# Where sequence 1's attention operands and squares are made: at the end of layer 0's second MLP product, or during the first blocks of q, k and v

## The chip, the cores and the metric

One Trainium2 chip, one core. The metric is the device time of one execution in microseconds (us), lower is better. The kernel before takes 1733.64 us, the median of three executions (1732.1 to 1736.89).

## The reference, cut to what matters

Two sequences, `x_prompt` and `x_sample` (each 512 tokens of 1024 features, fp32), go through the same trunk of two layers: a Fourier mixer and an MLP, then attention and an MLP. The place of interest is where layer 0 ends and layer 1's attention begins:

```python
def trunk(x, ...):
    x = x + fourier_mix(rms_norm(x, fourier_norm[0]), fourier_w_out[0])
    x = x + sq_relu_mlp(rms_norm(x, mlp_norm[0]), mlp_w_up[0], mlp_w_down[0])
    x = x + gqa_attention(rms_norm(x, attn_norm[0]), attn_w_qkv[0], ...)   # qkv = h @ w_qkv
    ...

def rms_norm(x, g):
    return x * rsqrt(mean(x * x, axis=-1) + EPS) * g
```

So each sequence needs the sum of its squares per token, and its activations times the gain `attn_norm`, before q, k and v are complete.

## The kernel before, in words

Activations are held transposed: features on the 128 partitions, 512 tokens along the row. `xt(q, fo)` is block `fo` (of 8) of sequence `q`, and the tile `xs[q, m]` holds the two blocks `2m` and `2m+1`. Every fp32 operand of a product is split into a high half and a low remainder, and each product is three matmuls (high by high, high by low, low by high). ScalarE (ACT) makes the high half and VectorE (DVE) the remainder: L82 and L83 for plain operands, L86 and L87 for operands that are scaled on the way.

The second MLP product of layer 0 (`second_product`) multiplies blocks of the hidden activations of both sequences by sums of weight blocks, in the manner of Strassen. Its last group runs over the output blocks `m` = 0 to 3. Each `m` is five products of 12 matmuls, in the order t1, t3, t2, b22, t4 (L818); DVE adds each one to the residual (L1065), then adds the shared part `e[m]` (L1229 for sequence 0, L1230 for sequence 1), and calls `ready(m)`. Meanwhile DVE also forms and splits the next block's weights (L1132 to L1140, L83). `late()` starts the loads and splits of the first four weight tiles of q, k and v.

`ready(m)` works for both sequences. For each of the two feature blocks, `make_h` writes the attention operand (the activation times the gain, as two halves: L86 on ACT, L87 on DVE), and `square` squares the block on ACT (L157) and adds it to a running sum on GpSimd (POOL, L159). `put_away` writes `xs[q, m]` to memory (`park`, L186, queue of SP).

The projection has three column groups: `cg` = 2 is k and v, 0 and 1 are q. A block `(cg, q, t)` is the product of 128 tokens `t` of sequence `q` by 512 columns, 8 feature blocks by 3 matmuls (L77 to L79). The four blocks `(2, 0, t)` are first done for feature blocks 0 to 5 (`begun`, 72 matmuls). Then `token_scale(0)` sums the squares over features with tiny matmuls (`sums`, L165) and takes the reciprocal root in small steps on DVE and ACT (L131 to L137). The loop then finishes the four blocks with feature blocks 6 and 7 (24 matmuls), and `token_scale(1)` is called after the first of them. Then come the blocks `(2, 1, t)`.

Each k/v block is finished on the other engines by one chain: ACT scales it out of PSUM (L1492), v is split (L86, L87), k is squared per head (L1380), its root is taken (L131 to L137), ACT applies it (L1397), DVE rotates it (L1403, L1406) and POOL adds the two parts (L1408). After the change these lines stand one lower or higher (L1493, L1379, L1396, L1402, L1405, L1407). The first transposes of k (L1418) stand before block `(2, 1, 2)`.

The order on each engine is not written out here. A scheduler places the instructions from the order in which the code issues them, and at run time each engine takes its own in that fixed order. Within the last group only the order of the matmuls is pinned by hand (`manual_schedule` with PE).

Of the kernel before, what the change touches and what calls it, by code (L numbers as in the profile page):

```python
# [21 lines left out]
NSEQ = 2  # L22
NT = S // P
KC = D // P
# [16 lines left out]
def trunk_kernel(ctx, tc, x_in, xt_in, y_out, dcos, dsin, feat, rope, gfour, gcol, grow, gfin,  # L41
# [19 lines left out]
    def slot(shape, dt):  # L61
        return act.tile(shape, dt, tag="u4", name=nm("u"))

    def tm(shape=(P, 512), dt=F32):
        return tmp.tile(list(shape), dt, tag="t2", name=nm("t"))
# [19 lines left out]
    def split_scaled(dst_hi, dst_lo, src, scale):  # L85
        nc.scalar.activation(dst_hi, src, AF.Copy, scale=scale)  # L86
        nc.vector.scalar_tensor_tensor(dst_lo, src, scale, f32(dst_hi), ALU.mult, ALU.subtract)  # L87
# [22 lines left out]
    def load_w(src, eng=nc.vector, parts=1, home=own):  # L110
        raw = load_raw(src)
        w = home()
        for i in range(parts):
            sl = slice(i * 1024 // parts, (i + 1) * 1024 // parts)
            split(w[0][:, sl], w[1][:, sl], raw[:, sl], eng)
        return w
# [32 lines left out]
    def xt(q, fo):  # L149
        return xs[q, fo // 2][:, fo % 2]  # L150

    def square(q, fo, n=512):

        if fo == 0:
            acc[q] = tm()
        s = tm() if fo else acc[q]
        nc.scalar.activation(s[:, :n], xt(q, fo)[:, :n], AF.Square)  # L157
        if fo:
            nc.gpsimd.tensor_add(acc[q][:, :n], acc[q][:, :n], s[:, :n])  # L159
# [17 lines left out]
    def make_h(q, fo, g0):  # L177

        h = slot([P, 2, 512], F32R)
        split_scaled(h[:, 0], h[:, 1], xt(q, fo), gc[:, g0 + fo : g0 + fo + 1])  # L180
        return h
# [3 lines left out]
    def put_away(q, i):  # L185
        nc.sync.dma_start(park[q, i], xs[q, i])  # L186
# [859 lines left out]
    def second_product(l, blocks, rows, late=lambda: None, ready=lambda m: None):  # L1046
# [179 lines left out]
        def finish(m):  # L1226
            left[m] -= 1
            if left[m] == 0:
                nc.vector.tensor_add(xs[0, m][:, 1], xs[0, m][:, 1], e[m])  # L1229
                nc.vector.tensor_add(xs[1, m], xs[1, m], e[m].unsqueeze(1).broadcast_to([P, 2, 512]))  # L1230
                ready(m)
# [100 lines left out]
    hT, rs, wkv = [[], []], [], []  # L1332

    def token_scale(q):
        r = sm.tile([P, NT], F32, tag="rs", name=nm("rs"), bufs=2)
        ss, room = sums(q)
        rsqrt(r, ss, NT, 1.0 / D, room)
        rs.append(r)
# [2 lines left out]
        for _ in range(2):  # L1341
            wkv.append(load_w(w_qkv[2, len(wkv)], home=lent))

    def ready(m):
        for q in range(NSEQ):
            for fo in range(2 * m, 2 * m + 2):
                hT[q].append(make_h(q, fo, KC))
                square(q, fo)
            put_away(q, m)

    second_product(0, blocks, rows, late, ready)

    gb = tm((P, 4, HD))
# [13 lines left out]
    def qkv(cg, q, t, ws, k0=0, k1=KC, o=None):  # L1367
        o = ps() if o is None else o
        cols = slice(t * P, (t + 1) * P)
        for k in range(k0, k1):  # L1370
            w = ws[k // 2]
            c = (k % 2) * 512
            mm3(o, hT[q][k][:, 0, cols], hT[q][k][:, 1, cols],
                w[0][:, c : c + 512], w[1][:, c : c + 512], k == 0, k == KC - 1)
        return o
# [7 lines left out]
    def norm_rope(raw, nh, table, ts, outs, ss=None, step=None, eng=nc.vector):  # L1383

        n = nh * len(ts)
        step = nh if step is None else step
        if ss is None:
            ss = small(n)
            head_squares(raw, 0, n, ss)
        r = small(n)  # L1390
        rsqrt(r[:, :n], ss[:, :n], n, 1.0 / HD)
        yield
        for h0 in range(0, n, step):
            t = ts[h0 // nh]
            x, t1, t2 = [tm((P, step, HD)) for _ in range(3)]
            for i in range(step):  # L1396
                nc.scalar.activation(x[:, i], raw[:, (h0 + i) * HD : (h0 + i + 1) * HD],  # L1397
                                     AF.Copy, scale=r[:, h0 + i : h0 + i + 1])

            def every(ap):  # L1400
                return ap.unsqueeze(1).broadcast_to([P, step, ap.shape[-1]])

            eng.tensor_mul(t1, x, every(table[:, 0, t]))  # L1403
            for b in range(2):
                sl, other = slice(b * 64, b * 64 + 64), slice(64 - b * 64, 128 - b * 64)  # L1405
                nc.vector.tensor_mul(t2[:, :, sl], x[:, :, other], every(table[:, 1, t, sl]))  # L1406
            for i in range(0, step, 2):  # L1407
                nc.gpsimd.tensor_add(outs[(h0 + i) // 2].rearrange("p (h d) -> p h d", h=2),  # L1408
                                     t1[:, i : i + 2], t2[:, i : i + 2])
            yield  # L1410
# [3 lines left out]
    def transpose_k(q):  # L1414
        for h in range(NKV):
            pt = ps()
            for t in range(NT):
                nc.tensor.transpose(pt[:, t * P : (t + 1) * P],  # L1418
                                    kr[q][:, t, h * HD : (h + 1) * HD], ident)
            kk = slot([P, 2, 512], F32R)  # L1420
            split(kk[:, 0], kk[:, 1], pt)
            kT[q, h] = kk

    def transpose_q(q, h):
        pt = ps()
        c = (h % 2) * HD
        for t in range(NT):
            nc.tensor.transpose(pt[:, t * P : (t + 1) * P], qr[q, h // 2][:, t, c : c + HD], ident)
        qT = slot([P, 2, 512], F32R)
        split(qT[:, 0], qT[:, 1], pt)  # L1430
        return qT
# [37 lines left out]
    for cg in (2, 0, 1):  # L1469
        ws = wkv if cg == 2 else [load_w(w_qkv[cg, u], home=own if u < 2 else lent) for u in range(4)]  # L1470
        for q in range(NSEQ):
            if cg == 2:
                vt[q] = (slot([P, NT, 256], F32R), slot([P, NT, 256], F32R))
                kr[q] = slot([P, NT, 256], F32)
            else:
                for i in range(2):
                    qr[q, 2 * cg + i] = slot([P, NT, 256], F32)
            for t in range(NT if (cg, q) != (1, 1) else 2):
                if (cg, q, t) in transposes:
                    transpose_k(transposes[cg, q, t])  # L1480
                if (cg, q, t) == (1, 1, 1):
                    first = transpose_q(0, 0)
                if (cg, q) == (2, 0):
                    o = qkv(cg, q, t, ws, KC - 2, KC, begun[t])
                else:
                    o = qkv(cg, q, t, ws)
                if (cg, q, t) == (2, 0, 0):
                    token_scale(1)
                r = rs[q][:, t : t + 1]
                if cg == 2:  # L1490
                    raw = tm((P, 256))
                    nc.scalar.activation(raw, o[:, :256], AF.Copy, scale=r)  # L1492
                    split_scaled(vt[q][0][:, t], vt[q][1][:, t], o[:, 256:], r)  # L1493
                    todo = norm_rope(raw, NKV, rt["k"], [t], [kr[q][:, t]])
                else:
                    raw = tm()
                    nc.scalar.activation(raw, o, AF.Copy, scale=r)
                    todo = norm_rope(raw, 4, rt["q"], [t], [qr[q, 2 * cg + i][:, t] for i in range(2)])
                for _ in todo:
                    pass  # L1500
# [324 lines left out]
```

## Time and profile before

| what | value |
|---|---|
| median of three executions | 1733.64 us |
| the profiled execution's own time | 1733.91 us |
| its span, first instruction to last | 1732.1 us |
| PE (TensorE matmuls) busy | 1696.8 us, 98% of the span |
| DVE, ACT, POOL busy | 1246.8, 858.1, 332.8 us |
| granted TensorE clock, mean | 0.996 of full speed |

In the rows of the profile a line begins with the start in us and the duration, then engine, line of the code, operation and tiles; `x12` is the number of instructions that were merged into the row, and the bracket at its end is the idle time of that engine before it and what ended it. PE is busy nearly all the time, so the time of the kernel is the work of PE plus the moments when PE waits.

### The profile page before, as it was taken

The numbers are of one execution on the slowest core, as the hardware profiler recorded it, in microseconds if no ns is written. First come the engines' busy times: TensorE is split into PE (matmuls) and PEld (weight loads), VectorE is DVE, ScalarE is ACT, GpSimd is POOL, SyncE is SP. The second block draws the span as 40 slices with busy tenths as digits, with TensorE's granted clock in tenths as the row PEclk, the third lists the DMA queues.
The fourth block names the chain that finished last, engine by engine and source line by source line (L and its number), as shares of the span: only waits on it lengthen the run. The fifth ranks groups of instructions, "written<-read, shape, count | busy, mean of one in ns | idle before, by whom it ended". The sixth has DMA issues, their size and how long they took to land. (4 is left out here: it accounts for less than half of the span.)

```text
span 1732.1 us, 21931 instructions
## 1 busy us (share of the span) xinstructions
PE 1696.8 (98%) x7855; PEld 1400.0 (81%) x7855; DVE 1246.8 (72%) x1840; ACT 858.1 (50%) x1516; POOL 332.8 (19%) x302
## 2 busy tenths in 40 slices
PE   8999999999999999999999999999999999999997
PEld 6887777888788888788877888788788888888886
DVE  7779777546877879975588834687755579787965
ACT  5666444445432435446687714654544554344234
POOL 1320443232000001322234303114332200000004
PEclk9999999999999999999999999999999999999999
DMA  9732555449653635421100213235543587465322
GB/s 316 197 120 100 182 183 177 147 173 346 238 206 122 213 131 203 162 88 38 36 25 1 98 49 122 103 108 182 185 158 140 198 311 257 145 213 193 119 74 97
DMA packets 103751, 266.59 MB, mean 154 GB/s; under 512 B 10185, under 2 KB 10185, under 8 KB 103642
## 3 DMA queue, kind: packets, MB, share of 16 engines
q1 hardware_dynamic: 87482, 233.21, 38.3%
q10 hardware_dynamic: 14112, 25.70, 3.9%
q0 software_dynamic: 2048, 6.29, 1.8%
q8 instruction: 61, 1.00, 0.2%
q14 instruction: 48, 0.39, 0.1%
HBM read 190.18 MB, written 73.92 MB: 152 GB/s over the span
## 5 line engine op out<-in xcount | busy, mean ns | idle before, releaser
L818 PE MATMUL ps<-u,w 128*128 128x512 f32 x4704 | 1079.3, 390 | 7.0 <-DVE w L83 5.0
L818 PEld LDWEIGHTS ps<-u,w 128*128 128x128 f32 x4704 | 883.3, 188 | 195.1 <-DVE w L83 7.4
L82 ACT CAST w<-raw 128x1024 fp32r<-128x1024 f32 (+1 forms) x226 | 220.8, 981 | 447.7 <-PE ps L818 272.4
L83 DVE TENSOR_TENSOR w<-raw,w 128x1024 fp32r<-128x1024 f32 (+1 forms) x226 | 263.7, 1169 | 72.2 <-ACT w L82 71.8
L159 POOL TENSOR_TENSOR t<-t,t 128x512 f32<-128x512 f32 (+1 forms) x56 | 80.2, 1435 | 732.8 <-ACT t L157 677.0
L83 DVE TENSOR_TENSOR u<-u,u 128x1024 fp32r<-128x1024 f32 x132 | 157.8, 1223 | 26.7 <-ACT u L82 26.1
L82 ACT CAST u<-u 128x1024 fp32r<-128x1024 f32 x132 | 132.3, 1044 | 70.0 <-PE ps L818 47.5
L77 PE MATMUL ps<-u,u 128*128 128x512 f32 (+2 forms) x388 | 150.2, 388 | 0.8 <-DVE u L83 0.4
L1065 DVE TENSOR_TENSOR u<-ps,u 128x512 f32<-128x512 f32 x160 | 109.9, 688 | 54.4 <-PE ps L818 53.8
L78 PE MATMUL ps<-u,u 128*128 128x512 f32 (+2 forms) x388 | 144.9, 373 | 1.1 <-DVE u L83 1.1
L79 PE MATMUL ps<-u,u 128*128 128x512 f32 (+2 forms) x388 | 144.4, 372 | 0.0
L818 PE MATMUL ps<-u,u 128*128 128x512 f32 x528 | 129.4, 396 | 8.3 <-DVE t L902 8.2
L818 PEld LDWEIGHTS ps<-u,u 128*128 128x128 f32 x528 | 98.8, 190 | 34.4 <-issue 7.8
L926 POOL TENSOR_TENSOR u<-u 128x512 f32<-128x512 f32 x28 | 36.5, 1304 | 421.9 <-ACT u L834 421.9
L83 DVE TENSOR_TENSOR u<-ps,u 128x512 fp32r<-128x512 f32 (+4 forms) x122 | 75.3, 635 | 19.5 <-ACT u L82 18.0
L78 PEld LDWEIGHTS ps<-u,u 128*128 128x128 f32 x388 | 73.4, 189 | 13.2 <-DVE u L83 3.1
L77 PEld LDWEIGHTS ps<-u,u 128*128 128x128 f32 x388 | 73.5, 190 | 12.2 <-ACT u L82 1.0
L79 PEld LDWEIGHTS ps<-u,u 128*128 128x128 f32 x388 | 73.1, 189 | 12.5
L82 ACT CAST u<-ps 128x512 fp32r<-128x512 f32 (+4 forms) x122 | 64.9, 548 | 25.4 <-PE ps L79 10.9
L801 DVE TENSOR_TENSOR u<-ps,u 128x512 f32<-128x512 f32 (+1 forms) x48 | 30.9, 645 | 64.7 <-PE ps L79 64.7
L891 DVE TENSOR_TENSOR t<-ps,u 128x512 f32<-128x512 f32 x30 | 20.7, 690 | 69.3 <-PE ps L818 64.0
L79 PE MATMUL ps<-u,w 128*128 128x512 f32 (+2 forms) x192 | 65.5, 341 | 2.5 <-DVE w L545 2.5
(233 smaller groups left out, 2006.6 us busy)
## 6 DMA issues: line engine op xcount, KB each, us to landing
raw<-w_up SPq DMA_DIRECT2D x82, 512.0 KB, 4.3
u<-spill_t SPq DMA_DIRECT2D x60, 512.0 KB, 6.1
raw<-w_sum SPq DMA_DIRECT2D x56, 512.0 KB, 3.8
u<-spill_b SPq DMA_DIRECT2D x45, 512.0 KB, 5.5
spill_t<-u SPq DMA_DIRECT2D x87, 256.0 KB, 2.0
spill_b<-t ACTq DMA_DIRECT2D x60, 256.0 KB, 2.9
raw<-w_row SPq DMA_DIRECT2D x28, 512.0 KB, 4.6
park<-u SPq DMA_DIRECT2D x24, 512.0 KB, 2.7
```

The source lines that it names most:

```text
L77: nc.tensor.matmul(out, lh, rh, start=first, stop=False)
L78: nc.tensor.matmul(out, lh, rl, start=False, stop=False)
L79: nc.tensor.matmul(out, ll, rh, start=False, stop=last)
L82: nc.scalar.copy(dst_hi, src)
L83: eng.tensor_sub(dst_lo, src, f32(dst_hi))
L159: nc.gpsimd.tensor_add(acc[q][:, :n], acc[q][:, :n], s[:, :n])
L801: nc.vector.tensor_add(x[:, :n], o[:, :n], x[:, :n])
L818: nc.tensor.matmul(o, w[x][:, sl], h[k][y], start=first and k + i == 0, stop=k == n - 1 and i == 2, skip_group_check=not first)
L891: nc.vector.tensor_add(u2, ob, t[:, 0])
L926: eng.tensor_sub(t[:, 0], b12, b11)
L1065: nc.vector.tensor_add(x, o, x)
```

## The change

`ready` takes the sequence as an argument and does sequence 0 alone at the end of the second product. For sequence 1 it is called from the projection's loop: after block `(2, 0, t)` it makes the operands, squares and write-out of tile `xs[1, t]`. `token_scale(1)`, which reads the sum of all squares of sequence 1, moves from after block `(2, 0, 0)` to after block `(2, 0, 3)`. No instruction of the computation is added or taken away.

```diff
-    def ready(m):
-        for q in range(NSEQ):
-            for fo in range(2 * m, 2 * m + 2):
-                hT[q].append(make_h(q, fo, KC))
-                square(q, fo)
-            put_away(q, m)
+    def ready(m, q=0):
+        for fo in range(2 * m, 2 * m + 2):
+            hT[q].append(make_h(q, fo, KC))
+            square(q, fo)
+        put_away(q, m)
...
                     o = qkv(cg, q, t, ws)
-                if (cg, q, t) == (2, 0, 0):
+                if (cg, q) == (2, 0):
+                    ready(t, 1)
+                if (cg, q, t) == (2, 0, 3):
                     token_scale(1)
```

DVE, at block m = 2 and the start of m = 3 of the last group. `u_5778` and `u_5784` are operands of sequence 1 (its tile is `u_3902`), `u_5771` is one of sequence 0. `w_5858` is the split weight that the first product of m = 3 waits for, `w_5934` that of its second product. Before:

```order
L87 SCALAR_TENSOR_TENSOR u_5771<-u_3679,gc,u_5771 128x512
L1134 TENSOR_TENSOR raw_5824<-raw_5824,raw_5822 128x512
L87 SCALAR_TENSOR_TENSOR u_5778<-u_3902,gc,u_5778 128x512
L87 SCALAR_TENSOR_TENSOR u_5784<-u_3902,gc,u_5784 128x512
L1065 TENSOR_TENSOR u_4019<-ps_5826,u_4019 128x512
L1140 TENSOR_TENSOR raw_5822<-raw_5822,raw_5854 128x512
L83 TENSOR_TENSOR u_5794<-raw_5791,u_5793 128x1024
L1065 TENSOR_TENSOR t_3745<-ps_5840,t_3745 128x512
L83 TENSOR_TENSOR u_5800<-raw_5797,u_5799 128x1024
L83 TENSOR_TENSOR w_5858<-raw_5854,w_5858 128x1024
```

After (the names are numbered anew: `u_5759` is sequence 0's operand, `w_5833` and `w_5896` are the two weights, `t_3745` and `u_4019` are sums of block m = 2):

```order
L87 SCALAR_TENSOR_TENSOR u_5759<-u_3679,gc,u_5759 128x512
L1134 TENSOR_TENSOR raw_5799<-raw_5799,raw_5797 128x512
L83 TENSOR_TENSOR u_5769<-raw_5766,u_5768 128x1024
L1065 TENSOR_TENSOR u_4019<-ps_5801,u_4019 128x512
L83 TENSOR_TENSOR u_5775<-raw_5772,u_5774 128x1024
L83 TENSOR_TENSOR w_5833<-raw_5829,w_5833 128x1024
L1065 TENSOR_TENSOR t_3745<-ps_5815,t_3745 128x512
L1140 TENSOR_TENSOR raw_5797<-raw_5797,raw_5829 128x512
L87 SCALAR_TENSOR_TENSOR u_5869<-u_3683,gc,u_5869 128x512
L83 TENSOR_TENSOR w_5850<-raw_5797,w_5850 128x512
L1065 TENSOR_TENSOR u_4019<-ps_5783,u_4019 128x512
L83 TENSOR_TENSOR w_5896<-raw_5799,w_5896 128x1024
```

The two operands of sequence 1 are gone from here, and the weight of m = 3 now stands ahead of the addition that reads the product t2 of m = 2 (`t_3745`) instead of behind it.

POOL, where layer 1 begins. `t_5626` is the running sum of squares of sequence 0, `t_5638` that of sequence 1 before and `t_6108` after; L1408 (after: L1407) is the last step of k for one block of tokens. Before:

```order
L159 TENSOR_TENSOR t_5626<-t_5626,t_6017 128x512
L159 TENSOR_TENSOR t_5638<-t_5638,t_6024 128x512
L159 TENSOR_TENSOR t_5638<-t_5638,t_6030 128x512
L1408 TENSOR_TENSOR u_6149<-t_6192,t_6193 128x256
L1408 TENSOR_TENSOR u_6149<-t_6227,t_6228 128x256
```

After:

```order
L159 TENSOR_TENSOR t_6108<-t_6108,t_6113 128x512
L1407 TENSOR_TENSOR u_6098<-t_6138,t_6139 128x256
L159 TENSOR_TENSOR t_6108<-t_6108,t_6155 128x512
L159 TENSOR_TENSOR t_6108<-t_6108,t_6161 128x512
L1407 TENSOR_TENSOR u_6098<-t_6186,t_6187 128x256
L159 TENSOR_TENSOR t_6108<-t_6108,t_6203 128x512
L159 TENSOR_TENSOR t_6108<-t_6108,t_6209 128x512
L1407 TENSOR_TENSOR u_6098<-t_6234,t_6235 128x256
L159 TENSOR_TENSOR t_6108<-t_6108,t_6251 128x512
L159 TENSOR_TENSOR t_6108<-t_6108,t_6257 128x512
L1407 TENSOR_TENSOR u_6098<-t_6297,t_6298 128x256
```

Six of the seven additions for sequence 1 now stand between the last steps of the four k blocks, the last two behind that of the third block.

PE, at the end of the k/v blocks of sequence 0. `ps_6157` (after: `ps_6262`) is the sum over features of sequence 1's squares, `ps_6308` is block `(2, 1, 0)`, the first of sequence 1. Before, with matmuls of the same kind left out:

```order
L165 MATMUL ps_6133<-ones,t_5626 128x2 x4
L77 MATMUL ps_6056<-u_5928,u_6008 128x512
...
L79 MATMUL ps_6056<-u_5928,u_6014 128x512
L165 MATMUL ps_6157<-ones,t_5638 128x2 x4
L77 MATMUL ps_6075<-u_5928,u_6008 128x512
...
L79 MATMUL ps_6113<-u_5928,u_6014 128x512
L77 MATMUL ps_6308<-u_5793,u_5635 128x512
```

After:

```order
L165 MATMUL ps_6082<-ones,t_5626 128x2 x4
L77 MATMUL ps_6005<-u_5890,u_5970 128x512
...
L79 MATMUL ps_6062<-u_5890,u_5976 128x512
L165 MATMUL ps_6262<-ones,t_6108 128x2 x4
L77 MATMUL ps_6308<-u_5768,u_6105 128x512
```

The tiny matmuls that read sequence 1's sum of squares move from behind the first finished block to the last place before block `(2, 1, 0)`, and they read the sum that POOL now completes behind the third k block.

## The prediction

> **What bounds the kernel now.** The page gives the busy time of the engines, and the waits of PE say what it waited for.
>
> ```profile
> PE 1696.8 (98%) x7855; PEld 1400.0 (81%) x7855; DVE 1246.8 (72%) x1840; ACT 858.1 (50%) x1516; POOL 332.8 (19%) x302
> ```
>
> ```profile
> PE ps L818 <- DVE w L83: 5.0, 4, 2.3
> PE ps L1418 <- POOL u L1408: 0.7, 1, 0.7
> ```
>
> PE is the bound everywhere, so any edit counts by what it adds to or takes from PE's waits. The timeline of PE shows the waits near the change.
>
> ```profile
> 671.62 44.81 PE L818 MATMUL ps<-u,w 128*128 128x512 f32 x197
> 717.95 3.01 PE L818 MATMUL ps<-u,w 128*128 128x512 f32 x12 [1.51 <-DVE w L83]
> 723.28 12.33 PE L818 MATMUL ps<-u,w 128*128 128x512 f32 x46 [2.32 <-DVE w L83]
> 735.45 0.39 PE L77 MATMUL ps<-u,u 128*128 128x512 f32 x1
> ...
> 751.77 0.95 PE L165 MATMUL ps<-ones,t 128*128 128x2 f32 x8
> 752.58 0.49 PE L77 MATMUL ps<-u,u 128*128 128x512 f32 x1
> ...
> 754.06 0.95 PE L165 MATMUL ps<-ones,t 128*128 128x2 f32 x8
> 754.87 0.48 PE L77 MATMUL ps<-u,u 128*128 128x512 f32 x1
> ...
> 758.82 0.39 PE L79 MATMUL ps<-u,u 128*128 128x512 f32 x1
> 759.04 0.39 PE L77 MATMUL ps<-u,u 128*128 128x512 f32 x1
> ```
>
> PE runs without a pause to 716.4, then waits twice, both times for a split weight of the last block, m = 3. `begun` starts at 735.45; its 72 matmuls end at 751.77, so a warm matmul takes 16.32 / 72 = 0.227. The sums stand at 751.77 and 754.06, and the 24 matmuls that finish the four blocks end at 759.04, where block (2, 1, 0) starts. The table by stage (length, PE busy, PEld, DVE, ACT, POOL, then granted clock) says what the waits did to the clock.
>
> ```profile
> 716.40:718.00 1.60, 0.09 (x2) 0.05 (x1) 1.60 (x2) 0.00 (x0) 0.42 (x1) 1.00 0.75 161
> 720.90:723.20 2.30, 0.07 (x1) 0.00 (x0) 2.30 (x4) 1.02 (x2) 0.00 (x0) 1.00 0.95 376
> 723.20:726.70 3.50, 3.42 (x9) 2.64 (x10) 3.50 (x5) 3.50 (x7) 3.14 (x2) 0.55 1.02 368
> 759.00:800.00 41.00, 40.31 (x186) 33.32 (x186) 26.06 (x95) 25.74 (x97) 7.32 (x10) 1.00 0.08 26
> ```
>
> DVE is busy through both waits, so its queue is the cause; behind the second one PE had 0.55 of its clock for 3.5 us. From 759 to 800 PE idles 0.69 in all: what is lost earlier cannot be won back there.
>
> **Term 1, the two waits go.** DVE's rows (701 to 724) show what stood ahead of the weights.
>
> ```profile
> 708.12 3.48 DVE L87 SCALAR_TENSOR_TENSOR u<-u,gc,u 128x512 fp32r<-128x512 f32 x2
> ...
> 715.60 2.30 DVE L83 TENSOR_TENSOR w<-raw,w 128x1024 fp32r<-128x1024 f32 x1
> ...
> 720.16 0.68 DVE L1065 TENSOR_TENSOR u<-ps,u 128x512 f32<-128x512 f32 x1
> 720.76 0.73 DVE L87 SCALAR_TENSOR_TENSOR u<-u,gc,u 128x512 fp32r<-128x512 f32 x1
> 721.42 0.68 DVE L1229 TENSOR_TENSOR u<-u,t 128x512 f32<-128x512 f32 x1
> 722.02 1.21 DVE L83 TENSOR_TENSOR w<-raw,w 128x1024 fp32r<-128x1024 f32 x1
> ```
>
> The L87 pair at 708.12 is sequence 1's and leaves. The split that ended the first wait (715.60) then stands ahead of the addition of t2 of m = 2, two products or more before PE needs it; the one that ended the second (722.02) moves ahead of L1065, L87 and L1229. Each then has over 3 us to spare, and what is late next is PE's own work. Without waits the 60 matmuls of m = 3 run from 716.28 (the last start of the first row plus 0.227) for 60 x 0.227 = 13.61, and `begun` starts at 729.89, not 735.45: **-5.56**. This is 1.51 + 2.32 of waiting and some 1.7 of slow clock. The loads of w_qkv follow their buffers' release, which comes earlier; SP writes sequence 1's tiles as before, by the same four transfers; one load of w_qkv now stands ahead of sequence 0's last write and of the load of the gains (L1354), which the rotation of the first k block needs, long after. If a weight is late after all, this term falls towards 0.
>
> The Trainium skill ("TensorE: Matmul & The Clock Gate", Part 1: The HAM clock gate) lets PE fall to half clock after an idle window of about 3.4 us; here it fell after 2.32, so the trace disagrees on the length, though a wait of 2.31 earlier in it left the clock at 1.00:
>
> ```profile
> 267.11 3.01 PE L818 MATMUL ps<-u,u 128*128 128x512 f32 x12 [2.31 <-DVE t L902]
> ```
>
> ```profile
> 267.20:271.00 3.80, 3.80 (x17) 1.00 0.84 299
> ```
>
> By the Trainium skill's window this term would be an estimated -3.83, the waits alone, and the sum 1.7 higher.
>
> **Term 2, PE now waits for sequence 1's squares.** PE takes its queue in order, and L165 for sequence 1 is the last item before block (2, 1, 0): every matmul of that block and all later ones are queued behind it. It waits for POOL's last L159, which stands behind the last step (L1407) of the third k block. That step ends a chain that begins when the first block leaves PSUM. Rows of before (ACT, then POOL):
>
> ```profile
> 754.31 0.47 ACT L1492 ACTIVATE t<-ps,rs 128x256 f32<-128x256 f32 x1 [0.75 <-PE ps L79]
> ...
> 758.61 0.46 ACT L1492 ACTIVATE t<-ps,rs 128x256 f32<-128x256 f32 x1
> ...
> 762.46 0.46 ACT L1492 ACTIVATE t<-ps,rs 128x256 f32<-128x256 f32 x1
> ```
>
> ```profile
> 767.15 0.74 POOL L1408 TENSOR_TENSOR u<-t,t 128x256 f32<-128x256 f32 x1 [2.93 <-DVE t L1406]
> ```
>
> The three blocks leave PSUM one after another, though PE has all of them by 759.04: the chain is serial on ACT, some 3.85 a block, and takes 767.89 - 754.31 = 13.58 to the end of the third L1408. Before, only the transposes at 771 waited for it. Its start moves with PE, to 754.31 - 5.56 = 748.75, so with nothing added it ends at 762.33. But sequence 1's work is now threaded into it:
>
> ```profile
> 704.63 0.72 ACT L86 ACTIVATE u<-u,gc 128x512 fp32r<-128x512 f32 x1 [3.83 <-DVE u L1229]
> 705.26 0.62 ACT L157 ACTIVATE t<-u 128x512 f32<-128x512 f32 x1
> 705.78 0.71 ACT L86 ACTIVATE u<-u,gc 128x512 fp32r<-128x512 f32 x1
> ```
>
> Start to start, L86 costs ACT 0.63 and L157 0.52. Between the first and the second block ACT has two of each: +2.30. Inside the second block's root DVE has four L87 (0.74 each, by the row at 720.76): +2.96. Between the second and the third block ACT has two L157: +1.04. Third step done: 762.33 + 6.30 = 768.63. Then POOL makes its last two L159, by the page's group
>
> ```profile
> L159 POOL TENSOR_TENSOR t<-t,t 128x512 f32<-128x512 f32 (+1 forms) x56 | 80.2, 1435 | 732.8 <-ACT t L157 677.0
> ```
>
> 2 x 1.435 = 2.87, to 771.50, and L165 takes 754.87 - 754.06 = 0.81. Block (2, 1, 0) starts at 772.31 instead of 759.04: **+13.27**, term 1 already in it. PE itself would have been there by 753.5, so it idles some 18 us.
>
> **Term 3, the clock.** After such an idle stretch PE restarts slow. By the stage table, 3.5 us at 0.55 cost 3.5 x 0.45 = **+1.58**; the least is 0 (the wait of 1.51 left the clock at 1.00).
>
> **Term 4.** The 0.69 wait of the transposes goes, since block (2, 1, 2) now starts some 12 us after L165 and the fourth chain needs about 5: **-0.69**. L1493 and the later squares wait for `token_scale(1)`'s root, but PE needs a further 5.4 for block (2, 1, 0) by then, which hides it.
>
> Sum: 13.27 + 1.58 - 0.69 = **+14.16**. Against the profiled execution, 1733.91 (span 1732.1 plus 1.81), this is 1748.1; it lies 0.27 above the median, so the median is forecast at 1733.64 + 14.16 = **1747.8**.
>
> **Bounds.** If the threaded work costs the chain nothing, 6.30 falls away: +7.86, or 1741.5. Upwards, DVE and POOL disturb each other. POOL's rows beside the L87 pair at 708.12 (3.48 for two, so 1.74 each, against 0.73 alone) and beside three in a row:
>
> ```profile
> 706.02 5.04 POOL L159 TENSOR_TENSOR t<-t,t 128x512 f32<-128x512 f32 x3 [13.41 <-ACT t L157]
> ...
> 739.94 5.20 POOL L159 TENSOR_TENSOR t<-t,t 128x512 f32<-128x512 f32 x3 [9.26 <-ACT t L157]
> ```
>
> Four L87 at 1.74 instead of 0.74 add 4.0, and two L159 at 5.20 / 3 = 1.73 add 0.6: +18.8, or 1752.4. I take the unlocked value, because in the order after, only two L159 stand beside those L87.
>
> The Trainium skill ("SBUF — State Buffer", Who interferes with whom) has the rule for this: a VectorE instruction with two SBUF inputs and a GpSimd one that reads SBUF exclude each other for a whole instruction. The 1.74 against 0.73 agrees. It speaks against this change, which moves both kinds into one serial chain.
>
> **Rivals.** 0.3% (5.2 us) is about what a measurement can tell from no change.
>
> - Forecast: PE waits for the threaded chain, 1745 to 1751. Chance 0.62.
> - The threaded work fits into the chain's own waits (ACT idles before each L1397, by the row below): 1741.5 to 1745. Chance 0.13.
>
> ```profile
> 758.01 0.70 ACT L1397 ACTIVATE t<-t,s 128x128 f32<-128x128 f32 x2 [1.08 <-DVE s L137]
> ```
>
> - DVE and POOL exclude each other all along the chain: 1751 to 1753.5. Chance 0.10.
> - Term 1 does not come, because another load or split of m = 3 is late: 14.16 + 5.56 = 19.7, so 1753.4. For it: DVE is busy 2.30 of 2.30 in that stage. Against: the weights now stand first. Chance 0.07.
> - Nothing measurable: the chain ends only some 6 us after PE is ready, and this cancels term 1. It would need the chain shorter than its bare 13.58. Chance 0.05.
> - The other side: the squares come in time. POOL would have to end its last L159 by 753.5, when PE is through with the 24 matmuls; from there on only terms 1 and 4 are left: -5.56 - 0.69 = -6.25, so 1727.4. For it: POOL is idle 81% of the span and the blocks xs[1, t] are complete long before. Against: the order on POOL puts two L1407 steps ahead of the last four additions. Chance 0.03.
>
> So slower 0.92, same 0.05, faster 0.03. The range from 1741.5 to 1754 leaves out about 1 in 10 on the two lower rivals and what lies above the late weight.
>
> **What would show it.** Right: no wait of PE on L83 between 716 and 736; `begun` some 5.6 earlier; one wait of PE at L165 of 15 to 20 us, released by POOL's L159; clock at about half for 3 to 4 us behind it; no wait at L1417. Wrong: a wait below 8 us at L165, a chain whose block period stays at 3.85, or waits on split weights that remain.

## The result and the profile after

The changed kernel takes 1753.54 us, the median of four executions (1752.16 to 1754.91), against 1733.06 (1732.1 to 1736.89) for the kernel before. The ratio is 1.0103, with a 95% interval of 1.0091 to 1.0115: slower by 1.0%, or 20.5 us. The forecast was slower by 14.2 us. The profiled execution after took 1754.18 us, with a span of 1752.4; the span before was 1732.1.

The list of PE's waits, after. Columns: what waited and for whom, then us in total, times, the longest one.

```profile
PE ps L165 <- POOL t L159: 19.8, 3, 18.8
...
PE ps L818 <- DVE u L1065: 1.8, 2, 1.1
...
PE ps L818 <- DVE w L83: 1.2, 2, 1.0
```

The waits on split weights fell from 5.0 to 1.2 (both waits at m = 3 are gone), the transposes' wait of 0.7 is gone too, and one wait of 18.8 us stands at the sums, released by POOL's addition of squares. It is also the last link of a chain that can be followed. First PE's timeline after:

```profile
731.18 3.02 PE L818 MATMUL ps<-u,w 128*128 128x512 f32 x12 [1.06 <-DVE u L1065]
734.03 0.39 PE L77 MATMUL ps<-u,u 128*128 128x512 f32 x1
...
775.71 1.87 PE L165 MATMUL ps<-ones,t 128*128 128x2 f32 x8 [18.80 <-POOL t L159]
777.43 0.78 PE L77 MATMUL ps<-u,u 128*128 128x512 f32 x1
```

`begun` starts at 734.03 and PE has all four blocks at 756.9 (775.71 - 18.80). Block (2, 1, 0) starts at 777.43, where it started at 759.04 before. The k chain on ACT, after: each block leaves PSUM at an L1493, and sequence 1's L157 and L86 stand between.

```profile
752.89 0.47 ACT L1493 ACTIVATE t<-ps,rs 128x256 f32<-128x256 f32 x1 [0.76 <-PE ps L79]
...
756.89 1.32 ACT L86 ACTIVATE u<-u,gc 128x512 fp32r<-128x512 f32 x2
758.12 0.61 ACT L157 ACTIVATE t<-u 128x512 f32<-128x512 f32 x1
758.64 0.45 ACT L1493 ACTIVATE t<-ps,rs 128x256 f32<-128x256 f32 x1
...
766.68 0.45 ACT L1493 ACTIVATE t<-ps,rs 128x256 f32<-128x256 f32 x1
...
771.27 1.13 ACT L157 ACTIVATE t<-u 128x512 f32<-128x512 f32 x2
772.31 0.45 ACT L1493 ACTIVATE t<-ps,rs 128x256 f32<-128x256 f32 x1
```

The steps from block to block are 5.75, 8.04 and 5.63 us. Before, by the prediction's rows, the first two were 4.30 and 3.85. POOL's queue after shows why PE has to see the third step done before its sums:

```profile
757.54 0.72 POOL L1407 TENSOR_TENSOR u<-t,t 128x256 f32<-128x256 f32 x1 [14.08 <-DVE t L1405]
758.22 3.38 POOL L159 TENSOR_TENSOR t<-t,t 128x512 f32<-128x512 f32 x2
766.74 0.72 POOL L1407 TENSOR_TENSOR u<-t,t 128x256 f32<-128x256 f32 x1 [5.14 <-DVE t L1405]
767.42 2.60 POOL L159 TENSOR_TENSOR t<-t,t 128x512 f32<-128x512 f32 x2
772.37 0.72 POOL L1407 TENSOR_TENSOR u<-t,t 128x256 f32<-128x256 f32 x1 [2.35 <-DVE t L1405]
773.05 2.60 POOL L159 TENSOR_TENSOR t<-t,t 128x512 f32<-128x512 f32 x2
```

The last squares (ACT) were there at 772.40 (771.27 + 1.13), but the additions begin at 773.05, behind the third L1407, and end at 775.65. The table by stage (length, PE, PEld, DVE, ACT, POOL, granted clock) for the restart:

```profile
775.70:777.40 1.70, 1.69 (x8) 1.70 (x9) 0.00 (x0) 0.00 (x0) 0.00 (x0) 0.50 0.00 0
777.40:780.90 3.50, 3.50 (x9) 2.80 (x10) 1.70 (x11) 1.82 (x9) 0.00 (x0) 0.51 0.00 0
781.00:800.00 19.00, 19.00 (x90) 15.82 (x89) 10.25 (x34) 8.90 (x29) 2.22 (x3) 1.00 0.18 55
```

PE runs at half clock for 5.2 us, and from 781 on nothing of the loss is won back.

Not all of the 20.3 us between the two profiled executions belongs to the change. Long ahead of it PE has a wait that is the same in both kernels. After, then before:

```profile
268.72 4.59 PE L818 MATMUL ps<-u,u 128*128 128x512 f32 x12 [2.32 <-DVE t L902]
273.15 2.23 PE L818 MATMUL ps<-u,w 128*128 128x512 f32 x9
```

```profile
269.96 5.38 PE L818 MATMUL ps<-u,w 128*128 128x512 f32 x23
```

The prediction shows the same 12 matmuls of before: 3.01 us from 267.11, behind a wait of 2.31. After the change they start 1.61 later (268.72 - 267.11), behind a wait of 2.32, and take 4.59, so that the next product starts 3.19 late (273.15 - 269.96), at a place that the change doesn't touch. The granted clock shows both parts: from 51 to 58 us its mean was 0.76 before and 0.56 after, and from 268.8 to 273 it was 1.00 before and 0.59 after. So what the change itself costs in this pair of profiles is read against an offset of 3.2.

### The profile page after: what moved, and what is told of

It reads as the page before. It is cut to its first block, busy times and chain, and to the rows that moved or that the text cites. A ratio compares the mean times of both kernels' runs of the same rounds, so it can differ in the third digit from the quotient of the medians.

```text
span 1752.4 us, 21934 instructions
## 1 busy us (share of the span) xinstructions
PE 1702.6 (97%) x7855; PEld 1403.6 (80%) x7855; DVE 1242.6 (71%) x1840; ACT 858.6 (49%) x1516; POOL 330.1 (19%) x302
## 5 line engine op out<-in xcount | busy, mean ns | idle before, releaser
L1065 DVE TENSOR_TENSOR u<-ps,u 128x512 f32<-128x512 f32 x160 | 109.7, 687 | 58.3 <-PE ps L818 57.6
```

The lines of the kernel that those rows point to most:

```text
L1065: nc.vector.tensor_add(x, o, x)
```

## The experiments

The theory (A): PE's wait comes from an order. Sequence 1's last additions stand on POOL behind the third rope step, and their squares on ACT behind the third block's steps; PE's sums wait for them with all later matmuls queued behind. The rivals: (C) the operands on ACT and DVE stretch the chain, and the squares matter little; (P) the later place of the sums costs by itself; (B, U, M) VectorE has no time for this work wherever it is put. Each ratio is to the kernel before on the same chip, whose medians in these comparisons were 1735.34 to 1736.42.

**Everything of sequence 1 ahead of the chain**, in one piece behind `begun`, sums where they were before:

```diff
+    for m in range(4):
+        ready(m, 1)
     token_scale(0)
...
-                if (cg, q) == (2, 0):
-                    ready(t, 1)
-                if (cg, q, t) == (2, 0, 3):
+                if (cg, q, t) == (2, 0, 0):
                     token_scale(1)
```

> Sequence 1's operands and squares are all made right after begun is issued, ahead of the first k/v block's chain, and its sums go back behind the first finished block. Theory A (PE waits because the work is threaded into the serial chain of the k blocks and the sums stand last): ACT's 8 L157 and 8 L86 (8 x 1.15 = 9.2 us) fit into the 9.0 us that ACT idles during begun, the wait of 18.8 us at L165 goes, and the saving on the two waits on split weights stays: 1728 to 1731 us, faster than before. Rival B (the changed place in time is what costs, wherever the work stands, because DVE or POOL lack the time there): a wait of 5 us or more at L165 or at the first block of sequence 1, 1735 or more.

Measured: 1740.2 us, ratio 1.0029 [1.0018, 1.0041]. The wait at the sums is gone, so some 13 us of the loss (1.0103 against 1.0029) come from the threading; but the gain didn't come either. PE waits for the keys instead, and DVE and POOL show why (waits, DVE, POOL of this kernel):

```profile
PE ps L1417 <- POOL u L1407: 6.2, 3, 3.3
```

```profile
743.38 8.99 DVE L1362 SCALAR_TENSOR_TENSOR u<-raw,t 128x128 f32<-128x128 f32 x16 [3.45 <-DMA t<-grow]
752.30 5.38 DVE L87 SCALAR_TENSOR_TENSOR u<-u,gc,u 128x512 fp32r<-128x512 f32 x8
```

```profile
739.30 11.92 POOL L159 TENSOR_TENSOR t<-t,t 128x512 f32<-128x512 f32 x8 [10.93 <-DVE w L83]
```

The 16 instructions of the rope tables (L1362) took 3.31 us in the kernel before, and 8.99 here, beside POOL's eight additions; the eight operand steps follow, and only then DVE can start sequence 0's root. My expectation held for the sums and failed for the time, where rival B was right. B had put the wait at the sums or at the first block of sequence 1, though; it stands at the keys.

**The squares alone ahead, the operands threaded**, sums behind the last block as in the changed kernel:

```diff
+    for fo in range(KC):
+        square(1, fo)
     token_scale(0)
...
-                    ready(t, 1)
+                    for fo in range(2 * t, 2 * t + 2):
+                        hT[1].append(make_h(1, fo, KC))
+                    put_away(1, t)
```

> As after, but the eight squares and seven additions of sequence 1 are made ahead of the chain; the operands (L86, L87) stay threaded and the sums stay last. Theory A: POOL's additions no longer stand behind the k blocks, so PE waits only for the operands, whose last one ended at 764.7 in the profile after, and ends its first block of sequence 1 some 18 to 20 us earlier: 1733 to 1737 us. Rival C (the four L87 inside the second root are the main cost): most of the wait stays, 1745 or more.

Measured: 1734.15 us, ratio 0.9992 [0.9983, 1.0001]. With the operands still threaded, nearly all of the loss is gone. Between 690 and 800 us PE's longest wait is 1.5.

**The operands ahead, the squares alone threaded**, the reverse:

```diff
+    for fo in range(KC):
+        hT[1].append(make_h(1, fo, KC))
     token_scale(0)
...
-                    ready(t, 1)
+                    for fo in range(2 * t, 2 * t + 2):
+                        square(1, fo)
+                    put_away(1, t)
```

> As after, but the eight operands are made ahead of the chain; the squares stay threaded and the sums stay last. Theory A: the chain loses two L86 (1.26 us) and four L87 in the second root (2.96), so PE's wait at L165 shrinks from 18.8 to about 14.6: 1749 us. Rival C (the operands are the main cost): 1738 or less.

Measured: 1750.83 us, ratio 1.0089 [1.0075, 1.0103]. Its longest wait, in the list of waits:

```profile
PE ps L165 <- POOL t L159: 17.1, 3, 16.1
```

The two together decide between A and C: the squares carry the loss, the operands 2.7 us of the wait (18.8 against 16.1), where 4.2 was expected.

**The sums one block later.** As the changed kernel, with one block of PE's work ahead of the sums:

```diff
-                if (cg, q, t) == (2, 0, 3):
+                if (cg, q, t) == (2, 1, 0):
                     token_scale(1)
```

> As after, but the sums of sequence 1's squares (L165) stand behind block (2, 1, 0) instead of ahead of it. Theory A: POOL's last addition ends as before, but PE does the 24 matmuls of that block (5.4 us) within the wait, as the operands come: 1748 us. Rival D (the operands, not the sums, hold PE): no gain, 1753; rival E (only the place of the sums costs): the wait goes, 1735 or less.

Measured: 1748.77 us, ratio 1.0074 [1.0058, 1.0089]; the wait at L165 is 10.4, and 1.7 on the operands come in its place:

```profile
PE ps L165 <- POOL t L159: 11.5, 3, 10.4
...
PE ps L79 <- DVE u L87: 1.7, 3, 0.8
```

Work of PE that is put ahead of the wait comes out of it, as A has it: the wait is 8.4 shorter, and the block's 5.4 with its own 1.7 of waits are 7.1 of that. One block is not enough.

**The place of the sums alone.** The kernel before, with only the second half of the change:

```diff
-                if (cg, q, t) == (2, 0, 0):
+                if (cg, q, t) == (2, 0, 3):
                     token_scale(1)
```

> The kernel before with one line moved: the sums of squares of sequence 1 (the call that leads to L165) stand behind block (2,0,3) instead of behind block (2,0,0); squares, additions and operands stay where they were, at the end of the second product. Theory A (what costs is that GpSimd's last additions of squares end late, not where TensorE's sums stand): the sums find their input ready, no wait at L165 over 1 us, time within 0.3% of the kernel before, ratio 0.997 to 1.003. Rival P (the place of the sums behind the last block of sequence 0 costs by itself, through ScalarE and VectorE steps of the scale that now stand inside the chain of rope steps): ratio 1.005 or more.

Measured: 1735.58 us, ratio 1.0002 [0.9992, 1.0011], no wait at the sums of sequence 1. Rival P is out.

**The gains loaded earlier**, so that the rope tables needn't wait for them; first with everything ahead of the chain, then with the squares alone:

```diff
     def late():
+        if not gains:
+            gains.append(tm((P, 4, HD)))
+            nc.sync.dma_start(gains[0], grow.to_broadcast([P, 4, HD]))
         for _ in range(2):
...
-    gb = tm((P, 4, HD))
-    nc.sync.dma_start(gb, grow.to_broadcast([P, 4, HD]))
+    gb = gains[0]
```

> As the kernel with all squares and operands of sequence 1 ahead of the chain (1740.2 us, ratio 1.0029), with one thing more: the load of the gains (grow) is issued at the first weight load of the second product's end instead of behind it. Theory T (the late gains held VectorE's rope tables for 3.45 us and so the chain): the tables start some 3 us earlier, the first scale of sequence 0 comes some 3 us earlier, about 1737, ratio 1.000 to 1.002. Rival U (the tables and GpSimd's additions share a path whatever the start, so the tables end where they ended): 1740, ratio 1.003 again.

> As the kernel with the squares alone ahead of the chain (1734.15 us, ratio 0.9992), and the load of the gains issued earlier as in the run before this one. Theory T: the tables start 4 us earlier and the chain with them some 3 us, about 1731, ratio 0.997 to 0.998. Rival U (they end where they ended): 1734, ratio 0.999 to 1.000.

Measured: 1740.66 us, ratio 1.0030 [1.0019, 1.0040], and 1733.68 us, ratio 0.9988 [0.9978, 0.9997]. The first shows the mechanism (DVE, then POOL, then the group of the table instructions with the shortest, median and longest one in ns; the tables are L1366 here):

```profile
741.93 12.12 DVE L1366 SCALAR_TENSOR_TENSOR u<-raw,t 128x128 f32<-128x128 f32 x16
```

```profile
741.39 12.12 POOL L159 TENSOR_TENSOR t<-t,t 128x512 f32<-128x512 f32 x8 [10.96 <-ACT t L157]
```

```profile
L1366 DVE SCALAR_TENSOR_TENSOR u<-raw,t x16: 277/826/1391, 741.9 to 753.8; 128x128 f32<-128x128 f32 x16
```

The tables start earlier, and last until POOL is through. In the kernel before the same group reads:

```profile
L1363 DVE SCALAR_TENSOR_TENSOR u<-raw,t x16: 276/279/282, 746.1 to 749.2; 128x128 f32<-128x128 f32 x16
```

Theory T (the late load) is out for the first kernel. For the second the interval overlaps that of the kernel without the early load, so the time decides nothing. Its trace speaks against T as well: the tables took 12.08 us beside 11.99 of additions (8.41 with the late load), and the first scale of sequence 0 came 19.02 behind the start of `begun` (753.39 - 734.37) instead of 19.62 (754.62 - 735.00), 0.6 earlier and not 3.

**The same two with sequence 1's additions on VectorE**, which takes the two engines apart, and the changed kernel with that edit alone:

```diff
-            nc.gpsimd.tensor_add(acc[q][:, :n], acc[q][:, :n], s[:, :n])
+            add_eng[q].tensor_add(acc[q][:, :n], acc[q][:, :n], s[:, :n])
...
     second_product(0, blocks, rows, late, ready)
+    add_eng[1] = nc.vector
```

> As the kernel with all squares and operands ahead of the chain and the gains loaded earlier (1740.66 us, ratio 1.003), with sequence 1's seven additions on VectorE instead of GpSimd. Theory L (VectorE's rope tables stand still while GpSimd adds): without six of GpSimd's eight additions there the 16 table instructions take 3.3 to 6 us instead of 12.12; the seven additions cost VectorE some 4.5 us; the first scale of sequence 0 comes 2 to 4 us earlier than 759.28, TensorE's waits on the keys' rope step fall from 6.4 to 2 to 4 us, ratio 1.000 to 1.002. Rival M (it is the amount of work ahead of the chain, whichever engine adds): tables and additions end where they ended, ratio 1.003 or more.

> As the kernel with the squares alone ahead of the chain and the gains loaded earlier (1733.68 us, ratio 0.9988), with sequence 1's additions on VectorE. Theory L: tables 3.3 to 6 us instead of 12.08, the first scale of sequence 0 some 2 us before 753.39. There TensorE waited only 0.3 us for the chain, so little of it reaches the end: 1733, ratio 0.998 to 0.999. Rival M: the same first scale or a later one, ratio 0.999 to 1.001.

> The changed kernel, with sequence 1's seven additions of squares on VectorE instead of GpSimd; everything else threaded as it is there. Theory A, fine form (the last squares themselves stand behind the third rope step on ScalarE, GpSimd's queue adds only its last steps): the last pair of squares still ends near 772.3, the additions behind it take about 1.3 us instead of 2.6 and no longer stand behind GpSimd's third addition of the rope step, so the wait at L165 falls from 18.8 to 15.5 to 17 us, ratio 1.007 to 1.0095. Rival Q (it is GpSimd's queue alone that holds the sums): the wait falls under 8 us, ratio 1.004 or less.

Measured, with everything ahead: 1736.85 us, ratio 1.0004 [0.9993, 1.0015]. PE no longer waits for the keys at all; 2.1 us at the sums, for DVE's last addition, are what is late next. DVE's row, and the one addition of sequence 0 that is left beside it on POOL (lines stand one to three lower in these kernels):

```profile
741.36 4.42 DVE L1368 SCALAR_TENSOR_TENSOR u<-raw,t 128x128 f32<-128x128 f32 x16
```

```profile
740.80 1.79 POOL L160 TENSOR_TENSOR t<-t,t 128x512 f32<-128x512 f32 x1 [10.91 <-ACT t L158]
```

4.42 us instead of 12.12, although DVE now makes seven additions more, behind the tables, and sequence 0's first scale comes at 755.22 instead of 759.28: theory L holds, and the amount of work (rival M) isn't what counts. With the squares alone ahead: 1733.3 us, ratio 0.9985 [0.9975, 0.9995]. That is a version that is a little faster than both kernels. The edit does more than these experiments are about: `add_eng[1]` stays set, so 14 additions of later stages move to VectorE as well, 21 in all, and near the kernel's end PE waits 1.68 for one of them in each of the three kernels (0.22, for POOL, in the one with the squares alone and the gains early). What this adds to the three times is not measured.

The changed kernel with the additions on VectorE: 1750.05 us, ratio 1.0092 [1.0067, 1.0116]. The interval overlaps that of the changed kernel; the trace tells more. PE's sums, ACT's last squares and DVE's last additions there:

```profile
771.69 1.87 PE L166 MATMUL ps<-ones,t 128*128 128x2 f32 x8 [15.89 <-DVE t L160]
```

```profile
768.88 1.13 ACT L158 ACTIVATE t<-u 128x512 f32<-128x512 f32 x2
```

```profile
769.82 1.82 DVE L160 TENSOR_TENSOR t<-t,t 128x512 f32<-128x512 f32 x2
```

From the last square to the last addition it is 1.6 us (771.64 - 770.01) instead of 3.25 (775.65 - 772.40), and the wait is 15.9 instead of 18.8. POOL's queue adds only its tail: most of the wait is the place of the squares themselves, behind the third rope step on ACT. Rival Q is out, and theory A is to be read as one chain over three engines.

**What held the weights (term 1).** Two kernels made from the one before. The first leaves sequence 1's pairs m = 0 and 1 where they were and makes m = 2 behind those of sequence 0's m = 3; the second makes only its m = 1 later, in the turn of m = 2:

```diff
-        for q in range(NSEQ):
-            for fo in range(2 * m, 2 * m + 2):
+        todo = [(0, m)]
+        if m < 2:
+            todo.append((1, m))
+        if m == 3:
+            todo += [(1, i) for i in (2, 3)]
+        for q, i in todo:
+            for fo in range(2 * i, 2 * i + 2):
```

```diff
-        for q in range(NSEQ):
-            for fo in range(2 * m, 2 * m + 2):
+        for q, i in [(0, m)] + {0: [(1, 0)], 1: [], 2: [(1, 1), (1, 2)], 3: [(1, 3)]}[m]:
+            for fo in range(2 * i, 2 * i + 2):
```

> The kernel before with only a quarter of sequence 1 moved: the operands and squares of its second-last pair of blocks (m = 2) are made behind those of the last pair of sequence 0, still at the end of the second product and ahead of the chain; nothing is threaded, the sums stay behind block (2,0,0). Theory A (TensorE's waits on split weights came from sequence 1's operands standing ahead of the splits on VectorE): the wait of 2.32 us at the last group goes, at least in part, the one of 1.51 stays, no wait at L165, ratio 0.998 to 0.9995. Rival V (VectorE has no time left ahead of the chain: two more operands and two more additions there push the rope tables and the first scale back): ratio 1.001 or more.

> The kernel before, with the operands and squares of sequence 1's second pair of blocks (m = 1) made behind those of its third pair's turn (m = 2) instead of in their own turn; nothing else moves. In the trace of before they are VectorE's two operand steps of 3.48 us at 708.12, beside GpSimd's three additions of 5.04 us. Theory A (these two steps and the additions beside them hold up the splits of the third group's weights, for which TensorE waits 1.51 and 2.32 us): both waits on the splits go, as they did in the changed kernel; in their place a wait of 1 to 3 us on VectorE's additions of the products (L1065) may come, since four operand steps now stand there; ratio 0.9985 to 1.001, the two waits gone is the test. Rival W (the splits wait for ScalarE's copies or for the weights' loads, whatever stands on VectorE): the waits of 1.5 and 2.3 us stay.

Measured, the first: 1736.18 us, ratio 1.0008 [0.9999, 1.0017]; the second: 1734.0 us, ratio 0.9984 [0.9973, 0.9995]. The row of the wait on split weights, first kernel, then the rows of the second:

```profile
PE ps L818 <- DVE w L83: 5.0, 4, 2.3
```

```profile
PE ps L1418 <- POOL u L1408: 1.4, 1, 1.4
PE ps L818 <- DVE u L1065: 1.3, 1, 1.3
PE ps L818 <- DVE w L83: 1.2, 2, 1.0
```

The first kernel keeps both waits: I had moved the wrong pair, as the steps of m = 2 stand on DVE behind the split that PE waited for. The second loses both (5.0 to 1.2) by moving two operand steps and two squares with their additions. So sequence 1's m = 1 held the weights, as the prediction has it; whether through the two operand steps on DVE (3.48) or through the additions on POOL that made DVE's steps longer, this does not separate. A new wait of 1.3 on DVE's addition comes, as in the changed kernel (1.06), and the rope step of the keys, not being earlier, costs 1.4. It is as fast as the best of the others, without any threading.

## Why the prediction was right, and where its sizes were off

| step | predicted | measured (profiled pair) |
|---|---|---|
| 1: both waits on split weights go, `begun` earlier | -5.56 | -4.6 (734.03 - 735.45 - 3.19) |
| 2: chain from its start to the third L1407's end | 19.88 | 20.20 (773.09 - 752.89) |
| 2: last two additions | 2.87 | 2.60 |
| 2: the sums, start to start | 0.81 | 1.72 |
| 2: block (2, 1, 0) later, net of term 1 | +13.27 | +15.2 (777.43 - 759.04 - 3.19) |
| 3: clock behind the wait | +1.58 | +1.7 (3.5 x 0.49) |
| 4: transposes' wait | -0.69 | gone, -0.9 (PE is 20.06 late ahead of them, 19.12 behind) |
| sum | +14.2 | +15.9 |

The mechanism was right: the two waits went, the sums took the place behind the chain, PE idled 18.8 where "some 18" was said, and the threaded work made the chain 6.6 longer (20.20 - 13.58) where 6.30 was said. The reason is tested: squares ahead of the chain take nearly all of the loss away, operands ahead don't, and the place of the sums alone costs nothing.

The time alone would not have told. 1753.54 lies above the forecast's own band of 1745 to 1751, where two of the rivals had put it (1751 to 1753.5, and 1753.4), and 0.5 us inside the end of the range. The trace decides against both rivals. The weights were not late, and the four operand steps in the second block's root, to be stretched to 1.74 each by VectorE and GpSimd excluding each other, took 0.74 or 0.75.

That 6.6 comes so near to 6.30 is partly luck. By parts, the prediction has +2.30 from the first block to the second, +4.00 (2.96 + 1.04) to the third, and nothing from there to the end of the third L1407. Measured are +1.45 (5.75 - 4.30), +4.19 (8.04 - 3.85) and +0.98 (6.41 - 5.43): a part that was too large hid one that had been put at nothing. In the third block two steps of the root on DVE lasted longer beside POOL's additions (767.42 to 770.02). L131 took 0.60 and L134 0.86, where the first block's took 0.17 and 0.16. The row at 720.76 also reads 0.73, not 0.74, which changes the sum by 0.04.

Two steps of the sum were too small. The first is "each then has over 3 us to spare, and what is late next is PE's own work". The weights had it, but DVE's addition of t3 hadn't: PE, now early, waits 1.06 for it, because two other splits stand ahead of it on DVE and met two of POOL's additions. Their rows after, DVE then POOL:

```profile
726.55 3.98 DVE L83 TENSOR_TENSOR u<-raw,u 128x1024 fp32r<-128x1024 f32 x2
```

```profile
725.40 4.04 POOL L159 TENSOR_TENSOR t<-t,t 128x512 f32<-128x512 f32 x2 [11.46 <-ACT t L157]
```

Two splits of 1.2 each had 3.98. So term 1 was 0.9 short. The second is the price of the sums, 0.81 by a row at full clock. They are the first matmuls behind the idle stretch, and run at half clock themselves: 0.9 more, a cost that term 3 began to count only behind them. The two make up 1.8 of the 1.9 by which block (2, 1, 0) missed its forecast.

The rest of the measured 20.5 us, some 4.6, isn't in the rows near the change. In the profiled pair, which differs by 20.3, 3.2 of it is the offset shown above, and 0.8 is the second of the two waits for DVE's L1065 in the list of PE's waits: 0.79 ahead of the matmuls at 1443.43, long behind the change. Whether the change causes that one is not shown. With the 15.9 that leaves 0.4. Offsets come without any change: in the kernel that moves the sums alone nothing is different up to `begun`, yet it starts at 740.39, 4.9 us behind 735.45. Three stretches of slow clock that before doesn't have account for nearly all of it: a clock of 0.57 from 86 to 90 and from 120 to 124, where before had 1.00, and 4.58 us for the same 12 matmuls behind a wait of 2.35 at 270.63.

```profile
728.40 12.14 PE L818 MATMUL ps<-u,w 128*128 128x512 f32 x46 [2.32 <-DVE w L83]
740.39 0.39 PE L77 MATMUL ps<-u,u 128*128 128x512 f32 x1
```

And the kernel before, 1733.06 in the comparison with the changed one, was 1735.34 to 1736.42 in the later ones. Against those the loss is 17 to 18. How much of the medians' 20.5 is such variation stays open: the changed kernel stands in one comparison only, and all four of its executions lie above 1752.

VectorE and GpSimd excluding each other had been priced for the four operand steps of the second root. In the chain it happened elsewhere: at the first pair of additions (3.38 for two, where the others took 2.60) and the first two operand steps beside it (2.85 for two), and at short steps of the root (L131 took 0.83 in the second block). It came in force ahead of the chain, in the experiments. DVE's rows after:

```profile
757.63 2.85 DVE L87 SCALAR_TENSOR_TENSOR u<-u,gc,u 128x512 fp32r<-128x512 f32 x2 [0.24 <-ACT u L86]
768.11 0.60 DVE L131 TENSOR_SCALAR s<-s 128x2 f32<-128x2 f32 x1
769.18 0.86 DVE L134 TENSOR_TENSOR s<-s 128x2 f32<-128x2 f32 x1
```

## What to carry to other kernels

Work that is moved into another stage's latency should be followed to its consumer on the busiest engine: here seven cheap additions came to stand at the end of a chain of three rope steps, and the in-order queue of PE stood behind it. Squares and sums are better finished ahead of such a chain, and only work with a late consumer (the operands) threaded into it. And here a wait was cured cheapest by moving only what stands ahead of it: to take two operand steps off VectorE's queue ahead of two splits, with their squares and additions, gave 0.16% [0.05, 0.27], where moving all of them lost 1.0%.

## What the hardware showed that was not expected

- **Turns of VectorE and GpSimd.** Beside GpSimd's additions, table instructions of 0.28 us took turns with additions: eight of the 16 took 0.28, and eight 1.37 to 1.39, each of these ending some 0.15 us behind the end of an addition. The 16 tables lasted 12.12 beside eight additions, or two tables per addition, 1.51 an addition. The Trainium skill ("SBUF — State Buffer", Who interferes with whom) has these two kinds exclude each other for a whole instruction, and the trace agrees. Every second table waited for an addition of 1.4 us, so these short instructions lasted as long as the additions did.
- **The clock behind short waits.** The same wait before the same 12 matmuls left them at 3.01 us in one execution (2.31 of idle) and 4.59 in another (2.32). Behind 18.8 us of idle, PE ran 5.2 us at 0.50 to 0.51. The Trainium skill ("TensorE: Matmul & The Clock Gate", Part 1: The HAM clock gate) lets the window of about 3.4 us run freely, not from the start of a kernel, so that the moment of a change varies; that two equal waits end differently agrees with it, that 2.3 us can be enough does not agree with its length.
